# Query products of RWKV-7 moved into the state steps, the second head pair in the other half of its output, scores of two pairs in one run

## The chip, the cores and the metric

The kernel runs on one core of a Trainium2 chip. The metric is the device time of one execution in microseconds. Three executions of the kernel before took 2675.3, 2671.83 and 2676.13 us, median 2675.3 us. TensorE is called PE below, VectorE DVE, ScalarE ACT, GpSimdE POOL and SyncE SP.

## The reference, cut to what matters

One decoder layer on 2048 tokens of width 1024 in float32: an RMS norm, one input projection, two mixers side by side (HGRN2 on four heads of 128, RWKV-7 on eight heads of 64), an output projection, and a ConvFFN. The change lies in the RWKV-7 mixer. Per head it computes

```python
def step(S, inp):
    rt, wt, kt, vt, at, bt = inp
    sa = jnp.einsum('bhvk,bhk->bhv', S, at)
    S = S * wt[:, :, None, :] + sa[..., None] * bt[:, :, None, :] + vt[..., None] * kt[:, :, None, :]
    y = jnp.einsum('bhvk,bhk->bhv', S, rt)
    return S, y
...
mu = jnp.mean(y, axis=-1, keepdims=True)
var = jnp.mean(jnp.square(y - mu), axis=-1, keepdims=True)
y = ((y - mu) * lax.rsqrt(var + RW_GN_EPS)).reshape(B, T, RW_WIDTH)
y = y * ln_w.astype(f32) + ln_b.astype(f32)
bonus = jnp.sum(heads(r * k * r_k.astype(f32)), axis=-1, keepdims=True) * heads(v)
y = y + bonus.reshape(B, T, RW_WIDTH)
return (y * g).astype(out_dtype)
```

`S` is a head's 64 by 64 state, `rt` the query, `ln_w` and `ln_b` the weight and bias of the group norm over a head's 64 channels.

## The kernel before

**Blocks and streams.** The tokens are cut into four blocks of 512. Phase 1 (projections and mixers, up to about 1345 us of the trace) is made of three Python generators: `dense` (the input and output projections, f32r products of 128 by 128 by 512 in triples at lines 263 to 265, named `pj`), `rw_super` (RWKV-7; eight calls, one for each block and each half of the heads) and `hg_unit` (HGRN2). One tick of the loop advances `rw_super` and `hg_unit` to their next `yield` and then lets `dense` issue about 2000 ns of work. So a `yield` in `rw_super` is a place where some nine dense matmuls go in. The framework then reorders the instructions of each engine a little by its own estimates, and each engine works through its queue in that order. Phase 2 (the last block's output projection, ConvFFN, final norm) has nothing of this.

**One call of `rw_super`** handles four heads, as two pairs `u` = 0, 1 of 128 channels each; a head `h` of a pair lies in partitions 64h to 64h+63. The 512 tokens are eight chunks of 64. The stages with the lines that the prediction names:

- L723, the scores: for each pair 16 small products (64 rows, 128 columns out, 128 tokens) in two groups `j`, each followed by a mask product on DVE (L726) into `M` and by a `yield` for each pair.
- L737 and L740 send pieces of `M` through DRAM into the layout `E`; L792 and L794 are 31 steps of a triangular inverse on DVE, L798 and L804 its transposes (`TZ`, `TTs`); L811, L824 and L837 bring the inverse together on PE.
- L857 starts the state sums `xp` in PSUM. L871 makes the chunk transition `G` and changes the queries `RT`. L871 walks over all four 64 by 64 quarters of the array: its `tile_position` is (64 or 0, 0 or 64).
- L884 starts the output sums `yp` in PSUM with the products inside a chunk.
- L894, the state steps: for each of eight chunks four products of `G` with the state `XH`, then DVE multiplies the result by the decay (L896) into the next `XH`, then a `yield`. The steps are a chain through DVE.
- L904, the query products: after the last step, 32 products of the states with `RT` are added into `yp`. Head `h` uses the quarter (64h, 64h).
- The group norm: square on ACT, two sums by the matrix `group` (L1060, L1061), Ln and Exp on ACT, one product on DVE (L916), then one ACT operation per pair with `ln_w` and `ln_b` (L918), the bonus `BV` (L926), the gate (L925 and L927) and the store to `oT` (L928).

A run below is a stretch of small matmuls on PE between two dense ones. An f32 matmul leaves two records in the trace, so a run of eight matmuls is shown as x16. The profile names PSUM tiles by their pools: `rw` for those of `rw_super` (`xp` and `yp` among them), `hg` for HGRN2 (L1032 is its state product).

**The start.** Before phase 1 all small parameter vectors are loaded as rows and transposed into `vt` (L153), and the first block's rows are normed: for each of four row tiles `nsq` and two `nst` operations on ACT (L118), then a product on DVE (L150), transposes on PE (L257), and `hh` and `hl` from them. Casts of the first weights (`wh`, L247) stand in the same ACT queue.

Of the kernel before, what the change touches and what calls it, by code (L numbers as in the profile page):

```python
# [7 lines left out]
F32 = mybir.dt.float32  # L8
# [3 lines left out]
AF = mybir.ActivationFunctionType  # L12
# [6 lines left out]
P = 128  # L19
# [45 lines left out]
def tile_layer(ctx, tc, consts, x, norm1_w, w_in, hg_lb_logits, hg_norm_w, rw_shift_mu, rw_w0, rw_w2,  # L65
# [4 lines left out]
    V, S, TE = nc.vector, nc.scalar, nc.tensor  # L70
    dma, store = nc.sync.dma_start, nc.gpsimd.dma_start

    cp = ctx.enter_context(tc.tile_pool(name="cp", bufs=1, reuse_waits="tile"))
# [36 lines left out]
    def act(out_, in_, func, **kw):  # L110

        want = tables.get(func)
        if want is not None and want != tab["now"]:
            pre = S.preload_act_table_set(want)
            for u_ in tab["uses"]:
                tc.add_manual_dep(pre.ins, u_.ins.name, NOSYNC, reason="table order")
            tab.update(now=want, pre=pre, uses=[])
        i_ = S.activation(out_, in_, func, **kw)  # L118
        if want is not None:
            tc.add_manual_dep(i_.ins, tab["pre"].ins.name, NOSYNC, reason="table order")  # L120
            tab["uses"].append(i_)
        return i_
# [11 lines left out]
    vt = cp.tile([P, P], F32, name="vt")  # L134
    off = {}
# [19 lines left out]
    def vec(nm, i):  # L155
        return vt[:, off[nm] + i:off[nm] + i + 1]


    lb = cp.tile([P, 12], F32, name="lb")
    lb0 = vt[:, off["lb"]:off["lb"] + 4]  # L160
# [106 lines left out]
    def phase1(c1):  # L267
# [353 lines left out]
        def last_dma(nb):  # L621

            return nc.gpsimd.dma_start if nb == NBLK - 1 else dma
# [14 lines left out]
        U = range(2)  # L638

        def rw_super(nb, s_):  # L640
# [75 lines left out]
            for j in range(2):  # L716
                for u in U:
                    s1 = bank2()
                    for i in range(4):
                        b, e = 2 * j + i // 2, i % 2  # L720
                        for h in range(2):
                            hr = slice(h * 64, h * 64 + 64)
                            TE.matmul(s1[:, h, i * P:i * P + P], KB[hr, 4 * u + b, 2 * e:2 * e + 2, :],  # L723
                                      AR[hr, u, :, 2 * b + e, :], start=True, stop=True)
                    for h in range(2):
                        V.tensor_mul(M[:, :, u, 2 * j:2 * j + 2, h, :].rearrange("p e b t -> p b e t"),  # L726
                                     s1[:, h].rearrange("p (b e t) -> p b e t", e=2, t=P),
                                     s1m.unsqueeze(1).unsqueeze(1).broadcast_to([P, 2, 2, P]))
                    yield

            E = rp.tile([P, 32, 32], F32, tag="E", name="E")
# [76 lines left out]
            for b, h, e, u in quads():  # L808
                r0 = er0(e)
# [70 lines left out]
            for u in U:  # L880
                for ch in range(8):
                    b, e = ch // 2, ch % 2
                    for h in range(2):
                        TE.matmul(yp[h * 64:h * 64 + 64, u, ch * 64:ch * 64 + 64],  # L884
                                  UV[:, 4 * u + b, e, h * 64:h * 64 + 64], M[:, e, u, b, h, 64:128], start=ch == 0,
                                  stop=False, tile_position=(0, h * 64), skip_group_check=True)
            WC2 = WC.rearrange("p (u c) t -> p u c t", u=2)
            for ch in range(8):
                b, e = ch // 2, ch % 2
                cs_ = slice(ch * 64, ch * 64 + 64)  # L890
                for u in U:
                    for h in range(2):
                        hr = slice(h * 64, h * 64 + 64)
                        TE.matmul(xp[hr, u, cs_], M[hr, 1, u, b, e, 0:64], XH[hr, u, ch, :], start=False,  # L894
                                  stop=ch == 7, tile_position=(h * 64, h * 64), skip_group_check=True)
                V.tensor_mul(XH[:, :, ch + 1, :], xp[:, :, cs_], WC2[:, :, ch].broadcast_to([P, 2, 64]))  # L896
                yield
            V.tensor_copy(Xc[:, 2 * s_:2 * s_ + 2, :], XH[:, :, 8, :])
            for u in U:
                for ch in range(8):  # L900
                    cs_ = slice(ch * 64, ch * 64 + 64)
                    for h in range(2):
                        hr = slice(h * 64, h * 64 + 64)
                        TE.matmul(yp[hr, u, cs_], XH[hr, u, ch, :], RT[hr, u, ch, :], start=False, stop=ch == 7,  # L904
                                  tile_position=(h * 64, h * 64), skip_group_check=True)
            yo = tile_("KB", [2, 2, BLK], "yo")
            y1, y2 = yo[:, 0], yo[:, 1]
            act(y1, yp, AF.Square)
# [5 lines left out]
            act(y1, b1, AF.Ln, bias=epsgn, scale=1.0 / 64)  # L914
            act(y1, y1, AF.Exp, scale=-0.5)
            V.tensor_mul(y2, yp, y1)  # L916
            for u in U:
                act(y2[:, u], y2[:, u], AF.Identity, bias=vec("lnb", prs[u]), scale=vec("lnw", prs[u]))  # L918
            yield
            while ("gd", nb) not in stage:  # L920
                yield None
# [1 line left out]
            gm = bank2()  # L923
            for u in U:
                TE.matmul(gm[:, u, :], g2[:, pc[u]], gdt, start=True, stop=True)  # L925
            V.tensor_add(y2, y2, BV)  # L926
            V.tensor_mul(y2, gm, y2)  # L927
            last_dma(nb)(oT[nb][512 + prs[0] * P:512 + (prs[1] + 1) * P, :].rearrange("(u p) t -> p u t", p=P), y2)  # L928
            done["rw2"] += 1
            yield  # L930

# [670 lines left out]
```

## Time and profile before

| | |
|---|---|
| median of three executions | 2675.3 us |
| profiled execution, its span | 2678.7 us |
| PE busy | 2595.9 us, 97% of the span |
| DVE busy | 1964.4 us, 73% |
| ACT busy | 1368.4 us, 51% |
| L904, 512 records | 18.8 us busy |
| L894, 512 records | 30.2 us busy |
| L723, 512 records | 37.9 us busy |

The profile is that of one execution, whose span lies 3.4 us above the median. A line of the timeline gives the start, the duration from the first start to the last end, the engine, the line, the operation, `out<-in`, the tile of the array in use, the moving shape and the number of records. Matmuls are pipelined, so durations overlap, and the distance between starts tells what a matmul costs its queue. A bracket at the end of a line is idle time ahead of it and who ended it.

### The profile page before, as it was taken

What the parts mean: (1) busy time and instruction counts of PE and PEld (TensorE: products, weight loads), DVE (VectorE), ACT (ScalarE), POOL (GpSimd) and SP (SyncE); (2) the same over time, 40 slices, a digit from 0 to 9 for tenths busy, and PEclk for the clock granted to TensorE, in tenths of its full rate; (3) what the DMA queues carried; (4) which work ended last, traced back from release to release, by engine and by line L of the source; (5) the groups of instructions that cost most, each with busy time, mean ns of one, the idle gap of its engine ahead of it and who ended that gap; (6) DMA issues with size and microseconds to landing.
All of it is one profiled execution on the core that took longest, in us unless ns stands there. A gap on an engine that the chain in (4) does not pass through costs nothing. (4 is left out here: it accounts for less than half of the span.)

```text
span 2678.7 us, 47929 instructions
## 1 busy us (share of the span) xinstructions
PE 2595.9 (97%) x18059; PEld 2089.1 (78%) x18059; DVE 1964.4 (73%) x3744; ACT 1368.4 (51%) x2200; POOL 383.2 (14%) x686
## 2 busy tenths in 40 slices
PE   7999999999999999999999999999999999999998
PEld 5877777777777777778778888887888888888887
DVE  4877767676567675667678789988998888676556
ACT  4556453554545455344457655456555545545444
POOL 6433222212222123222100000000000000000000
PEclk9999999999999999999999999999999999999999
DMA  8654443355643546844584458756754463898665
GB/s 301 202 164 165 163 142 116 115 162 183 201 152 115 153 157 221 277 131 129 172 287 139 138 188 262 239 172 194 260 199 150 149 203 124 318 322 280 204 193 185
DMA packets 312702, 510.54 MB, mean 191 GB/s; under 512 B 46879, under 2 KB 143509, under 8 KB 312469
## 3 DMA queue, kind: packets, MB, share of 16 engines
q1 hardware_dynamic: 257937, 329.13, 37.3%
q0 software_dynamic: 54464, 178.32, 20.4%
q8 instruction: 142, 2.33, 0.4%
q14 instruction: 91, 0.75, 0.1%
q10 hardware_dynamic: 68, 0.02, 0.0%
HBM read 373.13 MB, written 134.22 MB: 189 GB/s over the span
## 5 line engine op out<-in xcount | busy, mean ns | idle before, releaser
L263 PE MATMUL pj<-hh,wh 128*128 128x512 f32 x960 | 394.1, 411 | 6.7 <-ACT rkv L118 1.6
L264 PE MATMUL pj<-hl,wh 128*128 128x512 f32 x960 | 377.9, 394 | 0.0
L265 PE MATMUL pj<-hh,wl 128*128 128x512 f32 x960 | 377.7, 394 | 0.0
L263 PE MATMUL ua<-Bh,uwh 128*128 128x512 f32 x704 | 276.1, 392 | 3.8 <-ACT m L118 2.6
L265 PE MATMUL ua<-Bh,uwl 128*128 128x512 f32 x704 | 274.3, 390 | 0.0
L264 PE MATMUL ua<-Bl,uwh 128*128 128x512 f32 x704 | 274.1, 389 | 0.0
L263 PEld LDWEIGHTS pj<-hh,wh 128*128 128x128 f32 x960 | 181.1, 189 | 56.6 <-issue 9.1
L265 PEld LDWEIGHTS pj<-hh,wl 128*128 128x128 f32 x960 | 181.0, 189 | 39.6 <-issue 0.2
L264 PEld LDWEIGHTS pj<-hl,wh 128*128 128x128 f32 x960 | 181.3, 189 | 34.3 <-issue 0.6
L247 ACT CAST uwh<-uraw 128x512 fp32r<-128x512 f32 x220 | 135.2, 618 | 137.7 <-PE ua L264 63.3
L248 DVE TENSOR_TENSOR dal<-draw,dah 128x512 fp32r<-128x512 f32 x138 | 95.3, 690 | 111.3 <-ACT dah L247 110.0
L248 DVE TENSOR_TENSOR uwl<-uraw,uwh 128x512 fp32r<-128x512 f32 x220 | 147.5, 687 | 35.0 <-ACT uwh L247 34.9
L247 ACT CAST dah<-draw 128x512 fp32r<-128x512 f32 x138 | 85.9, 622 | 163.7 <-PE da L264 79.1
L263 PEld LDWEIGHTS ua<-Bh,uwh 128*128 128x128 f32 x704 | 132.1, 188 | 33.2 <-ACT m L118 4.8
L265 PEld LDWEIGHTS ua<-Bh,uwl 128*128 128x128 f32 x704 | 132.2, 188 | 28.1 <-DVE uwl L248 0.4
L264 PEld LDWEIGHTS ua<-Bl,uwh 128*128 128x128 f32 x704 | 132.2, 188 | 26.8
L263 PE MATMUL ud<-Bh,uwh 128*128 128x512 f32 x352 | 138.0, 392 | 0.0
L265 PE MATMUL ud<-Bh,uwl 128*128 128x512 f32 x352 | 137.0, 389 | 0.0
L264 PE MATMUL ud<-Bl,uwh 128*128 128x512 f32 x352 | 137.0, 389 | 0.0
L1472 POOL DMA_DIRECT2D gd<-y x2 | 1.1, 542 | 945.3 <-DVE y L1470 945.3
L264 PE MATMUL da<-dbl,dah 128*128 128x512 f32 x332 | 129.4, 390 | 0.3 <-DVE dbl L248 0.2
L265 PE MATMUL da<-dbh,dal 128*128 128x512 f32 x332 | 129.2, 389 | 0.0
(580 smaller groups left out, 6268.9 us busy)
## 6 DMA issues: line engine op xcount, KB each, us to landing
uraw<-in_w_up_dram SPq DMA_DIRECT2D x176, 256.0 KB, 3.3
woraw<-in_w_out_dram POOLq DMA_DIRECT2D x96, 256.0 KB, 3.4
br<-gd SPq DMA_DIRECT2D x88, 256.0 KB, 4.0
draw<-Sg SPq DMA_DIRECT2D x88, 256.0 KB, 2.8
draw<-Tw SPq DMA_DIRECT2D x88, 256.0 KB, 3.1
gd<-y SPq DMA_DIRECT2D x86, 256.0 KB, 2.8
Sg<-br SPq DMA_DIRECT2D x72, 256.0 KB, 2.1
xt<-x1d SPq DMA_DIRECT2D x32, 512.0 KB, 6.1
```

What stands on the lines that cost most here:

```text
L247: S.copy(hi, src)
L248: V.tensor_sub(lo, src, hi.bitcast(F32))
L263: TE.matmul(acc, lh, rh, start=first, stop=False, skip_group_check=skip)
L264: TE.matmul(acc, lh, rl, start=False, stop=False, skip_group_check=skip)
L265: TE.matmul(acc, ll, rh, start=False, stop=last, skip_group_check=skip)
L1472: (dma if end is None else nc.gpsimd.dma_start)(gd_[2 * h + b][fb * P:(fb + 1) * P, :], ys[0][:, b * BLK:(b + 1) * BLK])
```

## The change

Four things:

1. The `yield` of the scores stands behind both pairs of a group `j`, twice, in place of once behind each pair. The number of ticks stays.
2. The query products of a chunk stand right behind the four state products of its step.
3. Pair 1 writes its output sums `yp` into the other half of the partitions: head `h` of pair `u` goes to half `h ^ u`. This holds for L884 and for the query products, so that the four query products of a step use the four quarters of the array.
4. The group norm's last ACT operation brings pair 1 back: two operations of half height read one half of `y2` and write the other half of `y1`. Their weights and biases, swapped likewise, are copied once at the start into a small tile `lnx` by two ACT copies.

```diff
+    lnx = cp.tile([P, 4], F32, name="lnx")
+    for r0 in (0, 64):
+        S.copy(lnx[r0:r0 + 64, :], vt[64 - r0:128 - r0, off["lnw"] + 1:off["lnw"] + 8:2])
...
                         V.tensor_mul(M[:, :, u, 2 * j:2 * j + 2, h, :].rearrange("p e b t -> p b e t"),
                                      s1[:, h].rearrange("p (b e t) -> p b e t", e=2, t=P),
                                      s1m.unsqueeze(1).unsqueeze(1).broadcast_to([P, 2, 2, P]))
+                for _ in U:
                     yield
...
-                        TE.matmul(yp[h * 64:h * 64 + 64, u, ch * 64:ch * 64 + 64],
+                        c0 = (h ^ u) * 64
+                        TE.matmul(yp[c0:c0 + 64, u, ch * 64:ch * 64 + 64],
                                   UV[:, 4 * u + b, e, h * 64:h * 64 + 64], M[:, e, u, b, h, 64:128], start=ch == 0,
-                                  stop=False, tile_position=(0, h * 64), skip_group_check=True)
+                                  stop=False, tile_position=(0, c0), skip_group_check=True)
...
+                for u in U:
+                    for h in range(2):
+                        hr, c0 = slice(h * 64, h * 64 + 64), (h ^ u) * 64
+                        TE.matmul(yp[c0:c0 + 64, u, cs_], XH[hr, u, ch, :], RT[hr, u, ch, :], start=False,
+                                  stop=ch == 7, tile_position=(h * 64, c0), skip_group_check=True)
                 V.tensor_mul(XH[:, :, ch + 1, :], xp[:, :, cs_], WC2[:, :, ch].broadcast_to([P, 2, 64]))
                 yield
             V.tensor_copy(Xc[:, 2 * s_:2 * s_ + 2, :], XH[:, :, 8, :])
-            for u in U:
-                for ch in range(8):
-                    cs_ = slice(ch * 64, ch * 64 + 64)
-                    for h in range(2):
-                        hr = slice(h * 64, h * 64 + 64)
-                        TE.matmul(yp[hr, u, cs_], XH[hr, u, ch, :], RT[hr, u, ch, :], start=False, stop=ch == 7,
-                                  tile_position=(h * 64, h * 64), skip_group_check=True)
...
-            for u in U:
-                act(y2[:, u], y2[:, u], AF.Identity, bias=vec("lnb", prs[u]), scale=vec("lnw", prs[u]))
+            act(y1[:, 0], y2[:, 0], AF.Identity, bias=vec("lnb", prs[0]), scale=vec("lnw", prs[0]))
+            for r0 in (0, 64):
+                rs_ = slice(64 - r0, 128 - r0)
+                act(y1[r0:r0 + 64, 1], y2[rs_, 1], AF.Identity, bias=lnx[rs_, 2 + s_:3 + s_], scale=lnx[rs_, s_:s_ + 1])
...
-            V.tensor_add(y2, y2, BV)
-            V.tensor_mul(y2, gm, y2)
+            V.tensor_add(y1, y1, BV)
+            V.tensor_mul(y1, gm, y1)
```

In the changed kernel the lines stand a little lower: the dense triple is at 266 to 268, the scores at 726, the state steps at 899; the query products happen to be at 904 in both.

What this does to the order is shown at three places. The first is PE's queue at the scores of the second call of `rw_super` (rows of one instruction form each, `x8` means eight in a row). Before:

```order
L723 MATMUL rw<-AR,KB 128x128 x8
L263 MATMUL pj<-hh,wh 128x512
L264 MATMUL pj<-hl,wh 128x512
L265 MATMUL pj<-hh,wl 128x512
L263 MATMUL pj<-hh,wh 128x512
L264 MATMUL pj<-hl,wh 128x512
L265 MATMUL pj<-hh,wl 128x512
L263 MATMUL pj<-hh,wh 128x512
L264 MATMUL pj<-hl,wh 128x512
L265 MATMUL pj<-hh,wl 128x512
L723 MATMUL rw<-AR,KB 128x128 x8
```

With the change, from the first of the two runs on:

```order
L726 MATMUL rw<-AR,KB 128x128 x16
L266 MATMUL pj<-hh,wh 128x512
L267 MATMUL pj<-hl,wh 128x512
L268 MATMUL pj<-hh,wl 128x512
L266 MATMUL pj<-hh,wh 128x512
L267 MATMUL pj<-hl,wh 128x512
L268 MATMUL pj<-hh,wl 128x512
```

Four runs of eight score products with nine dense matmuls between them have become two runs of sixteen with eighteen between them.

The second place is PE's queue behind the last state step of the first call, where `hk` and `KT` are tiles of HGRN2. Before, the step and, nine dense matmuls later, the run of query products:

```order
L265 MATMUL pj<-hh,wl 128x512
L894 MATMUL rw<-XH,M 64x64 x4
L1021 MATMUL hg<-ident,hk 128x128 x4
L1023 MATMUL hg<-hX 64x64 x4
L263 MATMUL pj<-hh,wh 128x512
...
L264 MATMUL pj<-hl,wh 128x512
L265 MATMUL pj<-hh,wl 128x512
L904 MATMUL rw<-AR,XH 64x64 x32
L1032 MATMUL hg<-VT,KT 128x128 x4
L263 MATMUL pj<-hh,wh 128x512
```

With the change:

```order
L268 MATMUL pj<-hh,wl 128x512
L899 MATMUL rw<-XH,M 64x64 x4
L904 MATMUL rw<-AR,XH 64x64 x4
L1026 MATMUL hg<-ident,hk 128x128 x4
L1028 MATMUL hg<-hX 64x64 x4
L266 MATMUL pj<-hh,wh 128x512
...
L268 MATMUL pj<-hh,wl 128x512
L1037 MATMUL hg<-VT,KT 128x128 x4
L266 MATMUL pj<-hh,wh 128x512
```

The run of 32 is gone, and four query products stand in the step.

The third is ACT's queue at the start (`nsq` and `nst` belong to the norm of the input rows, `hh` to the first projected operand). Before:

```order
L247 CAST wh<-wraw 128x512
L118 ACTIVATE nst<-nst,eps_71 128x1
L118 ACTIVATE nsq,nst<-xt 128x1024
L118 ACTIVATE nst<-nst 128x1
L118 ACTIVATE ltmp<-ltmp 128x8
L118 ACTIVATE nst<-nst,eps_71 128x1
L247 CAST wh<-wraw 128x512
L118 ACTIVATE nst<-nst 128x1
L247 CAST wh<-wraw 128x512
L114 ACT_TABLE_LOAD
L118 ACTIVATE hh<-hg,vt 128x512 x2
```

With the change:

```order
L118 ACTIVATE nsq,nst<-xt 128x1024
L118 ACTIVATE ltmp<-ltmp 128x8
L250 CAST wh<-wraw 128x512
L118 ACTIVATE nst<-nst,eps_71 128x1
L250 CAST wh<-wraw 128x512
L118 ACTIVATE nst<-nst 128x1
L114 ACT_TABLE_LOAD
L498 CAST group<-cst 128x128
L118 ACTIVATE ones<-cst 128x128
L118 ACTIVATE hh<-hg,vt 128x512 x2
```

The last `nst` operation now stands behind both casts in place of between them, and two casts of constants have come ahead of `hh`.

More of the change, by code (lines that the diff above doesn't have):

```diff
@@ L925, in rw_super @@
                 TE.matmul(gm[:, u, :], g2[:, pc[u]], gdt, start=True, stop=True)
-            V.tensor_add(y2, y2, BV)
-            V.tensor_mul(y2, gm, y2)
-            last_dma(nb)(oT[nb][512 + prs[0] * P:512 + (prs[1] + 1) * P, :].rearrange("(u p) t -> p u t", p=P), y2)
+            V.tensor_add(y1, y1, BV)
+            V.tensor_mul(y1, gm, y1)
+            last_dma(nb)(oT[nb][512 + prs[0] * P:512 + (prs[1] + 1) * P, :].rearrange("(u p) t -> p u t", p=P), y1)
             done["rw2"] += 1
```

## The prediction

> **What bounds the kernel now.** I read the page first, then busy time by stages, then the matmul groups by line, and last TensorE's timeline around each place that the change touches.
>
> ```profile
> span 2678.7 us, 47929 instructions
> PE 2595.9 (97%) x18059; PEld 2089.1 (78%) x18059; DVE 1964.4 (73%) x3744; ACT 1368.4 (51%) x2200; POOL 383.2 (14%) x686
> ```
>
> ```profile
> 0.00:60.00 60.00, 43.51 (x185) 34.85 (x186) 28.67 (x64) 29.53 (x55) 37.87 (x67) 1.00 0.88 300
> 60.00:1290.00 1230.00, 1186.37 (x11490) 934.17 (x11492) 841.05 (x2006) 605.19 (x962) 321.88 (x577) 0.99 0.51 165
> 1290.00:1345.00 55.00, 50.19 (x591) 37.98 (x589) 37.43 (x80) 25.76 (x45) 8.26 (x15) 1.00 0.50 160
> 1345.00:2678.70 1333.70, 1315.82 (x5805) 1082.09 (x5803) 1057.22 (x1597) 707.87 (x1139) 15.15 (x28) 1.00 0.64 211
> ```
>
> The second fence is busy time by stage: length, then PE, PEld, DVE, ACT, POOL, the granted clock, DMA share, GB/s. The change sits in the mixer, which ends near 1345 us; the feed-forward behind it is untouched. From 60 to 1290 us PE is busy for 1186.4 of 1230 us (96%), DVE for 68%, ACT for 49%. PE's queue sets the pace there, so a microsecond of PE work taken out is a microsecond of time, unless PE then waits longer for somebody.
>
> PE's prices come from its timeline. First the dense projection, between whose matmuls all the others stand:
>
> ```profile
> 213.93 0.39 PE L263 MATMUL pj<-hh,wh 128*128 128x512 f32 x1
> ...
> 217.79 0.39 PE L265 MATMUL pj<-hh,wl 128*128 128x512 f32 x1
> ```
>
> These are 18 dense matmuls, so 17 steps in 3.86 us: 0.227 us each. The price of a run of small matmuls is the distance from the last dense start before it to the third dense start behind it, less three such steps (0.68 us).
>
> **The change part by part.**
>
> *Scores of both pairs in one run (L723).* A run of 16 records (eight matmuls; an f32 matmul leaves two records) and one of 32:
>
> ```profile
> 230.18 0.39 PE L265 MATMUL pj<-hh,wl 128*128 128x512 f32 x1
> 230.50 1.16 PE L723 MATMUL rw<-AR,KB 64*128 64x128 f32 x16
> ...
> 232.16 0.40 PE L265 MATMUL pj<-hh,wl 128*128 128x512 f32 x1
> ...
> 86.26 0.39 PE L264 MATMUL pj<-hl,wh 128*128 128x512 f32 x1
> 86.58 2.06 PE L723 MATMUL rw<-AR,KB 64*128 64x128 f32 x32
> ...
> 89.13 0.40 PE L264 MATMUL pj<-hl,wh 128*128 128x512 f32 x1
> ```
>
> Price of 16: 1.98 - 0.68 = 1.30 us. Of 32: 2.87 - 0.68 = 2.19 us. Two short runs cost 0.41 us more than one long one: a fixed price for leaving the full array and coming back. Counted in the instruction order of both kernels, separate runs of scores fall from 34 to 20 (13 of the 14 next to dense work). **14 x 0.41 = -5.7 us**; at least 13 of them are sure, since the run of 32 was itself measured.
>
> *The query products leave their own run (L904).* They stand with a state product behind them (L1032), whose own price is shown last:
>
> ```profile
> 191.30 0.40 PE L265 MATMUL pj<-hh,wl 128*128 128x512 f32 x1
> 191.63 2.08 PE L904 MATMUL rw<-AR,XH 64*64 64x64 f32 x64
> 193.64 1.16 PE L1032 MATMUL hg<-VT,KT 128*128 128x128 f32 x8
> ...
> 195.10 0.39 PE L265 MATMUL pj<-hh,wl 128*128 128x512 f32 x1
> ...
> 132.12 0.39 PE L265 MATMUL pj<-hh,wl 128*128 128x512 f32 x1
> 132.35 1.05 PE L1032 MATMUL hg<-VT,KT 128*128 128x128 f32 x8
> ...
> 133.70 0.39 PE L265 MATMUL pj<-hh,wl 128*128 128x512 f32 x1
> ```
>
> Together 3.80 - 0.68 = 3.12 us, L1032 alone 1.58 - 0.68 = 0.90 us, so the 64 query records cost 2.22 us. The last of them takes 0.22 us, so 63 steps fill 2.08 - 0.22 us: 0.0295 us a record, 1.89 us in all, and 0.33 us are the fixed price. Eleven such runs vanish in the order: **11 x 0.33 = -3.6 us**. Their 512 records were 512 x 0.0295 = 15.1 us.
>
> *They come back, four matmuls (eight records) in each of 64 state steps.* Each step is already a small run, so it brings no new fixed price:
>
> ```profile
> 177.99 0.39 PE L265 MATMUL pj<-hh,wl 128*128 128x512 f32 x1
> 178.31 0.45 PE L894 MATMUL rw<-XH,M 64*64 64x64 f32 x8
> ...
> 179.25 0.40 PE L265 MATMUL pj<-hh,wl 128*128 128x512 f32 x1
> ```
>
> A step costs 1.26 - 0.68 = 0.58 us. What eight more records add depends on how many quarters of the array work at once. Before, a query product of head h used quarter (h, h) for both pairs, so two quarters alternated at 0.0295 us a record. Now pair 1 uses (h, 1-h): four different quarters. The kernel has such a run, the products into G (L871), which walk all four:
>
> ```profile
> 156.76 0.69 PE L871 MATMUL rw<-M 64*64 64x64 f32 x32
> 157.27 0.65 PE L871 MATMUL rw<-KBT,M 64*64 64x64 f32 x32
> ```
>
> ```profile
> L904 PE MATMUL rw<-AR,XH 64*64 64x64 f32 x512 | 18.8, 220 | 0.0
> L871 PE MATMUL rw<-KBT,M 64*64 64x64 f32 x512 | 10.6, 221 | 0.0
> L896 DVE TENSOR_TENSOR XH<-rw,WC 128x128 f32<-128x128 f32 x64 | 18.5, 289 | 32.4 <-PE rw L894 31.7
> ```
>
> 32 records start within 0.51 us, 0.0159 us each, and by group 10.6 us stand against 18.8 us for equally many records of equal shape. I take 0.0159, the row with the same four quarters: 512 x 0.0159 = 8.1 us, **net 8.1 - 15.1 = -7.0 us**. Upper bound: no overlap at all, twice 0.0295, 30.2 us and net +15.1. Lower bound: below nothing there is no mechanism, but wholly hidden where PE waits for the step's DVE product, net -15.1.
>
> The Trainium skill, "TensorE: Matmul & The Clock Gate" (section "Wait — 56ns, not 53.3ns?"), says that matmul starts never come closer than about 25 ns however small the matmul is. By that rule 512 records cost 12.8 us (an estimate) and the move saves 2.3 us, not 7.0. The L871 rows, 15.9 ns a record, speak against it if a record is a start, and for it if two records are one start (31.8 ns), which these rows don't tell.
>
> The chain inside the steps is not lengthened by a wait: the DVE product of a step (L896) waits for the four state products, and the query products stand behind these. They can delay only the next thing on PE, a dense matmul.
>
> *The ACT tail.* Two scalings of a 512-column row become one full and two half-height ones:
>
> ```profile
> L118 ACT ACTIVATE yo<-yo,vt 128x512 f32<-128x512 f32 x16 | 12.2, 811 | 3.5 <-DVE yo L916 3.5
> L118 ACT ACTIVATE M<-rw 64x512 f32<-64x512 f32 x16 | 9.5, 593 | 0.3
> ```
>
> 12.2/16 = 0.76 us becomes 2 x 0.59 = 1.19, so +0.43 us in eight stages, 3.4 us on an engine that is busy 49%. Behind it stand two DVE products and a store; the dense work between hides it. **0**, or +3.4 if that cover were gone.
>
> *The start.* Two tiny copies on ACT reorder its queue there: the cast that now ends at 19.10 comes ahead of the last row scale.
>
> ```profile
> 17.84 0.20 ACT L118 ACTIVATE nst<-nst 128x1 f32<-128x1 f32 x1
> 18.48 0.62 ACT L247 CAST wh<-wraw 128x512 fp32r<-128x512 f32 x1 [0.44 <-DMA wraw<-in_w_in_dram]
> 20.41 1.27 ACT L118 ACTIVATE hh<-hg,vt 128x512 fp32r<-128x512 f32 x2
> 18.07 0.75 DVE L150 TENSOR_SCALAR xt<-xt,nst 128x1024 f32<-128x1024 f32 x1 [2.21 <-ACT nst L118]
> ```
>
> The scale moves from 17.84 to about 19.1, the DVE scaling (L150) behind a weight product to about 19.8 and so 1.7 us late; of that the table load ahead of hh already covers some, while two constant casts (0.4 us) now stand ahead of hh. hh starts near 21.2 in place of 20.41: **+0.8 us**, between 0 and 1.7.
>
> *Where it could stall anew.* Both pairs' scores come up to nine dense matmuls earlier, and the order pulls the next consumers forward. The tight place is L811, which needs DVE's transpose TZ:
>
> ```profile
> 1276.22 1.05 DVE L798 STREAM_TRANSPOSE TZ<-Ti 128x512 f32<-128x512 f32 x1
> 1277.35 0.75 PE L811 MATMUL rw<-TZ,M 32*32 32x32 f32 x64
> ```
>
> TZ ends 0.08 us ahead of L811: no room. Dense matmuls between the last score and L811, by stage: 139, 147, 132, 125, 129, 129, 150, 149 before; 138, 150, 141, 129, 135, 126, 172, 137 now. The last stage loses 12 (2.7 us), the sixth 3 (0.7 us); the masks of the second pair end a bit later after the last score too, some 0.6 us. I put **+4 us**, between 0 (the chain shortens as well) and 8 (twice that).
>
> Sum: -5.7 - 3.6 - 7.0 + 0.8 + 4 = **-11.5 us**. The profiled execution (2678.7) becomes 2667; it lies 3.4 us above the median, so the median of 2675.3 becomes **2664**.
>
> **The rivals.**
>
> *The quarters don't overlap in so short a group.* Eight records behind eight of the old pattern cost 0.0295 each: the term of -7.0 is 0, the sum -4.5, 2671. For it: L871's row is a long steady run, a step's is not. Against: nothing in the four products depends on each other. With the page's 25 ns it would be 2668.5, an estimate. Chance 0.14.
>
> *PE merely arrives early.* Some waits of PE are set by chains, not by its own work:
>
> ```profile
> PE rw L857 <- ACT M L118: 10.1, 7, 2.2
> ```
>
> If every stage is paced by its chain of scores, DVE inverse and state, what PE saves turns into longer waits like these and the time stays within 0.2%: 2675. Against it: the waits named on L857 are 10.1 us in all, and dense work is what fills the rest. Chance 0.12.
>
> *Slower through L811.* The order is pulled forward in every stage but the inverse is not faster: if each of eight stages waits 2.7 us as I expect of the last, that is 21.6 us against 16.3 us saved, with the start +6: 2681. It decides from 1.9 us a stage (15.5/8) on. For it: no room at TZ. Against it: five of eight stages have more dense work in between than before. Chance 0.08.
>
> *More than summed.* No new stall, and the earlier finish of the query sums shortens waits: -17, 2658. Chance 0.10.
>
> **How the numbers follow.** The forecast has 0.56. A time can be told from no change here beyond about 0.2%, 5.4 us. Faster: 0.56 + 0.10 and about 0.11 out of the first two rivals, 0.77. Same: 0.15. Slower: 0.08. The range takes in the larger gain (2658, less 2 us for the spread of single executions) and reaches to within 3 us of no change: 2656 to 2672; the likeliest case alone spans 2659 to 2669.
>
> **What would show it.** Scores in runs of 32 records with 2.2 us around them. A step of 16 records that costs 0.70 us rather than 0.58 (the quarters work) or 0.82 (they don't). No run of L904 of 64 records. A wait of PE for TZ in the last stage near 3 us, and the first dense matmul near 22.0 rather than 21.15 us. I am wrong if PE's idle time in the mixer grows by more than 10 us, or if steps grow by more than 0.25 us each.

## The result, and the profile after

Measured together, seven executions each: the changed kernel 2666.8 us median (2659.8 to 2670.3), the kernel before 2676.1 (2671.8 to 2684.0). The ratio is **0.996, interval [0.9943, 0.9976]**. Two later measurements of the changed kernel gave 0.9956 [0.9942, 0.997] and 0.9955 [0.9941, 0.9969]: by the ratios 10 to 12 us faster. The forecast was 2664.0 us, 11.5 us less than before, with a range of 2656 to 2672; the measured 2666.8 lies inside it. Three executions of the experiments at a granted clock of 0.56 to 0.85 took 2858 to 4212 us and stand in none of the ratios.

The page of the kernel after, its span and busy times:

```profile
span 2664.2 us, 47925 instructions
PE 2583.5 (97%) x18059; PEld 2085.9 (78%) x18059; DVE 1966.5 (74%) x3744; ACT 1374.6 (52%) x2210; POOL 381.6 (14%) x686
```

Its busy time by stage, with the columns of the same table of before. The mixer now ends near 1330 us in place of 1345:

```profile
0.00:60.00 60.00, 44.46 (x191) 35.41 (x192) 29.09 (x66) 30.53 (x58) 38.63 (x68) 1.00 0.87 308
60.00:1275.00 1215.00, 1173.96 (x11532) 929.60 (x11530) 842.82 (x2004) 608.44 (x967) 319.11 (x574) 0.98 0.50 166
1275.00:1330.00 55.00, 49.64 (x534) 39.38 (x534) 37.08 (x78) 25.04 (x42) 8.06 (x15) 0.94 0.51 164
1330.00:2664.20 1334.20, 1315.42 (x5806) 1081.49 (x5804) 1057.53 (x1598) 710.58 (x1145) 15.82 (x29) 1.00 0.64 211
```

The last row is the feed-forward: 1334.2 us against 1333.7, so the difference lies in the mixer. The column behind POOL's has changed too: the granted clock is 0.98 and 0.94 in the two stages of the mixer, where before it stood at 0.99 and 1.00.

For an account of the mixer I cut its span (first dense matmul to the first projection of phase 2) into windows of 1 us and split PE's time in three: busy time multiplied by the granted clock ("work"), idle time, and the rest of busy time ("lost to the clock"). One profiled execution each, in us:

| kernel | work | idle | lost to the clock | sum |
|---|---|---|---|---|
| before | 1264.5 | 48.4 | 11.3 | 1324.2 |
| changed, first profile | 1241.8 | 46.4 | 22.2 | 1310.4 |
| changed, second | 1243.9 | 46.5 | 15.9 | 1306.3 |
| changed, third | 1242.7 | 45.6 | 14.8 | 1303.1 |

Work fell by 21 to 23 us, idle time by 2 to 3, and the clock took 4 to 11 back. The profiled execution of before was longer than most of that kernel's: the time of an execution is 1.8 us above its span, so it took some 2680.5 us, against medians of 2673.1 to 2676.1. Differences between single profiles therefore overstate the gain by some 4 to 7 us.

What the change does is there in PE's timeline, first a run of scores, then a state step with its query products:

```profile
84.83 0.39 PE L267 MATMUL pj<-hl,wh 128*128 128x512 f32 x1
85.15 2.06 PE L726 MATMUL rw<-AR,KB 64*128 64x128 f32 x32
...
87.70 0.40 PE L267 MATMUL pj<-hl,wh 128*128 128x512 f32 x1
...
172.43 0.39 PE L268 MATMUL pj<-hh,wl 128*128 128x512 f32 x1
172.75 0.39 PE L899 MATMUL rw<-XH,M 64*64 64x64 f32 x6
172.93 0.27 PE L904 MATMUL rw<-AR,XH 64*64 64x64 f32 x2
172.97 0.23 PE L899 MATMUL rw<-XH,M 64*64 64x64 f32 x2
173.03 0.28 PE L904 MATMUL rw<-AR,XH 64*64 64x64 f32 x6
...
173.81 0.40 PE L268 MATMUL pj<-hh,wl 128*128 128x512 f32 x1
```

With the three dense steps, 0.68 us together, taken off, as in the prediction, the run of 32 costs 2.19 us and the step 1.38 - 0.68 = 0.70 us. These two are typical: of the runs and steps that stand alone between dense matmuls at full clock, eleven runs have a median of 2.19 us and 30 steps one of 0.70.

Three of the waits of PE in the mixer, by line (total, times, longest, in us); the first had 10.1 us before, the third 0.5:

```profile
PE rw L861 <- ACT M L118: 8.3, 5, 4.2
PE pj L266 <- ACT hh L243: 7.2, 7, 2.0
PE rw L815 <- DVE TZ L802: 2.4, 3, 2.0
```

### The profile page after: what moved, and what is told of

Its sections match the earlier page's. It is cut to its first block, busy times and chain, and to the rows that moved or that the text cites. A ratio compares the mean times of both kernels' runs of the same rounds, so it can differ in the third digit from the quotient of the medians.

```text
span 2664.2 us, 47925 instructions
## 1 busy us (share of the span) xinstructions
PE 2583.5 (97%) x18059; PEld 2085.9 (78%) x18059; DVE 1966.5 (74%) x3744; ACT 1374.6 (52%) x2210; POOL 381.6 (14%) x686
## 4 chain that ended last, share of the span: by engine, by line
PE 50%; DMA 6%; DVE 5%; ACT 3%; issue 2%; SPq 0%; DVEq 0%; POOL 0%; ACTq 0%; POOLq 0%
PE ua L266 5%; PE ua L268 5%; PE ua L267 5%; PE da L266 3%; PE da L267 3%; PE da L268 3%; PE ud L268 2%; PE ud L267 2%; PE ud L266 2%; PE pj L266 2%; PE pj L267 2%; PE db L268 2%; PE db L266 2%; PE db L267 2%; PE pj L268 2%
```

## The experiments

**One part at a time.** Four kernels, measured side by side. The first has only the merged scores:

```diff
-                    yield          # behind each pair u
+                for _ in U:        # behind both pairs
+                    yield
```

> The kernel before with the one yield edit: scores of both pairs in one run, query products as before. Fixed-price theory (my forecast): separate runs of scores fall from 34 to 20 and each saves 0.41 us, so 5.7 us of TensorE work go; with up to 4 us of new waits at L811 the time is 2 to 6 us below the kernel before, ratio 0.998 to 0.9993, and runs of 32 records cost 2.19 us. Rival, TensorE merely arrives early: ratio 1.000, TensorE's idle time in the mixer grows by some 6 us. Rival of the slowed clock (seen in the profile after): the work falls by 5.7 us, but the granted clock decides each single execution; kernels with the same work spread over about 10 us with the clock between 0.989 and 0.995.

Measured: ratio 0.9997 [0.9985, 1.0009]. The price per run was as forecast, yet no change of the time can be told: the interval reaches from 4 us less to 2 us more. PE's idle time in the profile did not grow, as the rival would have it, but fell from 48.4 to 45.7 us.

The second has everything but the other output half (so neither `lnx` nor the third ACT operation): the query products stand in the steps, on quarter (h, h).

> The changed kernel without the swap: query products in the state steps and scores in one run, but both pairs of the output sums in the same half, so a head's two query products use the same quarter; the small weight tile and the third ACT operation go too. Quarter theory: a step costs about 0.82 us in place of the 0.70 of the changed kernel and the 0.58 of the one before, 64 x 0.12 = 7.5 us more than the changed kernel; ratio to the kernel before 0.998 to 0.9995. Rival, the quarters give nothing in so short a group: a step costs the same 0.70 us, and the time is that of the changed kernel, 0.996.

Measured: 0.9966 [0.9952, 0.9979], faster than my theory said (0.998 to 0.9995) and close to the rival's 0.996. Its steps, however, cost what the theory said:

```profile
171.20 0.39 PE L265 MATMUL pj<-hh,wl 128*128 128x512 f32 x1
171.52 0.45 PE L895 MATMUL rw<-XH,M 64*64 64x64 f32 x8
171.80 0.40 PE L900 MATMUL rw<-AR,XH 64*64 64x64 f32 x8
...
172.70 0.40 PE L265 MATMUL pj<-hh,wl 128*128 128x512 f32 x1
```

1.50 - 0.68 = 0.82 us (also the median of 28 such steps), the forecast's figure for quarters that do not work. The swapped half is worth 0.12 us a step and 64 x 0.12 = 7.7 us of PE's queue. In the time it brought 0.9966 - 0.9956 = 0.1%, some 2.7 us, with intervals that overlap: the 7.7 us are shown in PE's queue, not in the time.

The third has everything but the merged scores.

> The changed kernel with the yield edit undone: query products in the steps with four quarters, scores in separate runs as before. Forecast: 3.6 us for eleven runs and 7.0 us for the quarters stay, 5.7 us are lost, so 4 to 10 us below the kernel before, ratio 0.9965 to 0.9985. Rival, TensorE merely arrives early: 1.000 here and in the run with the scores alone. If new waits come from the scores' order (L811 pulled forward), TensorE's idle time in the mixer is smaller here than in the changed kernel.

Measured: 0.9991 [0.9979, 1.0003]: 2.4 us less, where I had expected 4 to 10, and again no change that can be told. Idle time was larger here than in the changed kernel (51.9 against 46 us), so the scores' order does not bring it new waits on the whole.

> The changed kernel once more, beside the others on the same chip. Forecast theory: 0.996 as first measured. Theory of the slowed clock: its executions spread over some 10 us and follow the granted clock, about 2658 at 0.995 and 2668 at 0.990, and those of the kernel before spread likewise; at equal clock the distance is 15 us or so.

Measured: 0.9956 [0.9942, 0.997]. So the parts alone give 0.8 us (scores) and 2.4 us (queries with the other half), and both at once 11.8 us. In work the parts do add up:

| kernel | work | idle | lost to the clock | sum |
|---|---|---|---|---|
| scores only | 1256.4 | 45.7 | 10.6 | 1312.7 |
| without the other half | 1253.7 | 45.0 | 6.2 | 1304.9 |
| scores apart | 1251.4 | 51.9 | 9.9 | 1313.2 |

Scores alone take off 8.1 us of work, the rest alone 13.1, together 21.2; the whole change took off 20.6 to 22.7. What does not add up must lie in idle time and the clock, though the differences between these rows are hardly larger than what single profiles are off by. The idle time comes next.

**A wait that grew.** In the second stage PE waits for ACT's `M` 1.67 us before and 4.20 us after. It is 3.69 us with the scores merged alone and 1.93 with them apart, so it comes with the merged scores. (Over all stages this wait did not grow: 10.1 us before, 8.3 to 9.2 in the three profiles of the changed kernel.) My first theory was that dense work is missing there, since the ticks around the scores had changed. I moved one tick from the scores to the place of the wait:

```diff
-                for _ in U:
+                for _ in range(j + 1):
                     yield
...
+            yield
             for u in U:          # L861, the state sums
```

> The changed kernel, with one of the four score yields (the one behind both pairs of j = 0) taken away and one put right ahead of the state sums (L861 of the changed kernel, which wait for ACT's M). In the order, dense matmuls between L841 and L861 go from 12, 12, 12, 9, 10, 6, 12, 12 per stage to 18, 14, 18, 6, 18, 9, 10, 18, and separate tile runs from 195 to 189. Theory: the idle time that the merged scores left at L861 (4.20 us in the second stage, 8.3 us over all stages) mostly goes, and with it the stretch of lowered granted clock behind it (300 to 310 us of the trace; such an event costs 1.7 us, the half of 3.4): work at full clock in the mixer falls by a further 2 us (6 runs fewer at 0.41), idle time there by about 5, the clock's share by 2, in all 5 to 10 us below the changed kernel run beside it. Rival: the idle time is set by a chain and only moves to the next consumer (the inverse or the first state step): within 3 us of the changed kernel.

Measured: ratio 1.0013 [1.0004, 1.0022], slower than the kernel before and 15 us behind the changed kernel beside it.

> The kernel before with the scores of both pairs in one run and, as in the run with the moved yield, one of the four score yields put ahead of the state sums; the queries stand in their own run as before. Separate tile runs 202 (before 220, scores merged alone 207). Theory: what the merged scores alone did not bring (ratio 0.9997 where 5.7 us were due) was eaten by the wait at L857 and its lowered clock, so with that wait covered the time is 5 to 9 us below the kernel before. Rival: the merged scores bring nothing at all however they are covered: within 3 us of the kernel before.

Measured: 1.0062 [1.005, 1.0074], some 17 us worse than the merged scores alone (0.9997). The theory fell in both, and so did its rival, which allowed a difference of 3 us. In the first, work stayed as in the changed kernel (1242.0 us) and idle time rose to 65.9; in the second, work stayed near that of the merged scores (1255.5) and idle time rose to 61.4. PE's waits in the first of the two:

```profile
PE rw L876 <- DVE AR L882: 10.9, 5, 3.9
PE rw L862 <- ACT M L118: 8.7, 6, 2.8
...
PE rw L726 <- DVE M L729: 4.4, 6, 1.0
```

The wait for `M` did not shrink (8.7 against 8.3 us over all stages), and two new ones appeared: the scores now wait for their mask on DVE, and the second pair's `G` waits for DVE's `AR`. The tick between the score groups had covered the one; the other is explained by the next reading.

> The changed kernel once more, to stand beside the others on the same chip: 10 to 14 us below the kernel before, with stretches of lowered clock near 220, 300, 580 or 645, 920, 1120 and 1295 us if these are tied to places in the order.

Measured: 0.9955 [0.9941, 0.9969], with lowered clock at 216, 298, 575, 643, 909 and 1288 us: most of the places came back, none near 1120.

**Who holds it up.** The timeline of all engines in the second stage, before:

```profile
295.14 0.33 SPq L1055 DMA_DIRECT2D oT<-osq  x1
297.82 2.21 PE L837 MATMUL rw<-RHS,TTs 64*64 64x128 f32 x62
300.67 0.43 DVE L936 TENSOR_SCALAR hk<-hf 128x512 f32<-128x512 f32 x1 [4.12 <-DMA oT<-osq]
301.13 0.44 ACT L118 ACTIVATE hX<-hk 128x256 f32<-128x256 f32 x1 [2.07 <-DVE hk L936]
301.58 2.41 ACT L118 ACTIVATE UV<-rw 64x512 f32<-64x512 f32 x4
304.65 2.09 PE L857 MATMUL rw<-UV,KBT 128*64 128x64 f32 x64 [1.67 <-ACT M L118]
```

And after:

```profile
292.11 2.35 PE L841 MATMUL rw<-RHS,TTs 64*64 64x128 f32 x62
292.34 0.33 SPq L1060 DMA_DIRECT2D oT<-osq  x1
297.62 0.43 DVE L941 TENSOR_SCALAR hk<-hf 128x512 f32<-128x512 f32 x1 [2.87 <-DMA oT<-osq]
298.08 0.45 ACT L118 ACTIVATE hX<-hk 128x256 f32<-128x256 f32 x1 [2.37 <-DVE hk L941]
298.55 2.40 ACT L118 ACTIVATE UV<-rw 64x512 f32<-64x512 f32 x4
300.96 1.82 ACT L118 ACTIVATE M<-rw 128x512 f32<-128x512 f32 x3
301.61 3.68 PE L861 MATMUL rw<-UV,KBT 128*64 128x64 f32 x64 [4.20 <-ACT M L118]
```

Read it from below. The state sums read `UV` and `KBT`; what they wait for is that ACT's first copy into `M` empties the PSUM bank that they write. `M` stands behind `UV` in ACT's queue, and `UV` behind `hX`, which belongs to HGRN2 and has nothing to do with RWKV. `hX` waits for DVE's `hk`, and `hk` shares its buffer with `osq`, the output of the HGRN2 unit before, whose store is still under way: 5.3 us from its issue (292.34) to `hk` (297.62). The products that `UV` reads end at 300.0 us before and at 294.5 after, 5.6 us earlier; `UV` starts only 3.0 us earlier. The missing 2.5 us are the longer wait. In the kernel with the moved tick the same store holds `hk` for 4.49 us in the seventh stage, with DVE's `AR` behind it, and PE waits 3.85 us for `AR`.

Three kernels test this by taking the store's source out of that buffer. The last product goes into the gate's own tile:

```diff
-            V.tensor_mul(sq, sq, gg)
-            last_dma(nb)(oT[nb][j * P:(j + 1) * P, :], sq)
+            V.tensor_mul(gg, sq, gg)
+            last_dma(nb)(oT[nb][j * P:(j + 1) * P, :], gg)
```

> The changed kernel, with HGRN2's gated output written into the gate's own tile and stored from there, so that the next unit's hk no longer waits for the store of osq. Theory: in the second stage PE's wait for ACT's M (4.2 us) is made in ACT's queue: UV stands behind hX, hX waits 2.4 us for DVE's hk, and hk waits 2.9 us for the store of osq, while the products that UV reads had ended 4 us before. With the store out of the way DVE's waits for it (6.0 us over four places) are gone, UV starts 3 to 4 us sooner, PE's wait there falls to 1 us or less, and the lowered clock at 300 us (1.7 to 3.4 us) goes with it: 3 to 7 us below the changed kernel. Rival: UV is held by something else in ACT's queue, or the saved wait comes back at the next consumer: within 2 us of the changed kernel.

Measured: 2654.1 us median, ratio **0.9931 [0.9917, 0.9946]**, where the changed kernel has 0.9955 to 0.996. The second stage:

```profile
292.25 2.36 PE L841 MATMUL rw<-RHS,TTs 64*64 64x128 f32 x62
292.48 0.33 SPq L1060 DMA_DIRECT2D oT<-hgg  x1
292.49 0.43 DVE L941 TENSOR_SCALAR hk<-hf 128x512 f32<-128x512 f32 x1
293.68 0.44 ACT L118 ACTIVATE hX<-hk 128x256 f32<-128x256 f32 x1
296.22 2.41 ACT L118 ACTIVATE UV<-rw 64x512 f32<-64x512 f32 x4
299.30 2.09 PE L861 MATMUL rw<-UV,KBT 128*64 128x64 f32 x64 [1.72 <-ACT M L118]
```

`hk` no longer waits, `UV` starts 2.3 us earlier, PE's wait is 1.72 in place of 4.20 us (I had expected 1 us or less), and the state sums take 2.09 us rather than 3.68. What still stood ahead of `UV` in ACT's queue is the norm of the next rows, which ended at 296.20 us. This is the fastest kernel here; it was not measured beside the changed kernel, only both against the kernel before, and the intervals still overlap by a little.

> The kernel before with the scores of both pairs in one run and nothing else of the change, and HGRN2's output stored from the gate's tile. Theory: the merged scores alone brought nothing (ratio 0.9997) because the wait behind the store ate them; with it gone they bring what their runs cost: 4 to 7 us below the kernel before with the same store. Rival: what eats them is elsewhere: the two are within 2 us.

> The kernel before with HGRN2's output stored from the gate's tile, nothing else. DVE's waits for the store (6.1 us over three places) go, PE's wait for M in the second stage (1.67 us) shrinks. Both theories: 0 to 3 us below the kernel before, since the products that UV reads end late there and the store holds them up less.

Measured: 0.9967 [0.9954, 0.998] and 0.9979 [0.9967, 0.999]. So the buffer alone is worth 5.7 us on the kernel before, twice what I expected, and 7 to 8 us with the merged scores. But the two stand only 2.7 us apart, between my theory (4 to 7) and its rival (2), with intervals that overlap: the wait behind the store is a real loss in every version, and it does not by itself explain why the merged scores alone brought nothing. The profiles show where the gain lies: without the store PE's wait for `M` over all stages falls from 10.1 to 3.8 us in the kernel before, from 8.5 to 5.1 with the merged scores and from 8.3 to 5.0 in the changed kernel.

**The clock.** The other part that did not add up. In the changed kernel the clock falls near the end of that wait and stays low behind it (same columns as the table by stage):

```profile
298.00:301.00 3.00, 0.00 (x0) 0.00 (x0) 2.92 (x9) 2.86 (x6) 0.70 (x2) 0.91 0.89 324
301.00:304.00 3.00, 2.39 (x44) 2.40 (x46) 0.42 (x1) 1.74 (x3) 0.00 (x0) 0.50 0.12 45
304.00:307.00 3.00, 3.00 (x90) 2.88 (x86) 0.00 (x0) 0.00 (x0) 0.00 (x0) 0.50 0.00 0
```

To see whether the wait causes it, I gave PE something to do there:

```diff
+            if (nb, s_) == (0, 1):
+                for _ in range(56):
+                    TE.matmul(xp[:, 0, 0:P], group, ones, start=True, stop=True, skip_group_check=True)
             for u in U:          # L861, the state sums
```

> The changed kernel, with 56 constant products of 128 x 128 (the group matrix by ones, 3 to 3.5 us of PE, into the bank of the state sums, whose first products overwrite them) right ahead of L861 in the second stage alone, where PE waits 4.20 us for ACT's M. Their results are used by nothing. Theory (the granted clock falls because PE has been idle): the wait shrinks to about 1 us, the stretch of lowered clock at 300 to 310 us reads 1.00, the other stretches stay, and the time is equal or 1.7 to 3.4 us shorter although 3 us of work were added. Rival (the lowered clock has nothing to do with idle time, it comes with the work or by chance): the stretch stays at 300 to 310 us, and the time is equal or up to 3 us longer.

Measured: 0.9985 [0.9972, 0.9999], 8 us slower than the changed kernel. It tested nothing of what it was meant for, because the added products waited themselves (the view ends at 312 us, with 54 of the 56):

```profile
300.44 11.78 PE L859 MATMUL rw<-ones,group 128*128 128x128 f32 x54 [4.42 <-ACT M L118]
```

They write the bank that ACT's `M` has to empty first. So PE was as idle as before, and 12 us of work at the lowered clock (0.22 us a product) followed. It did show that the bank alone, without the data, makes PE wait as long. The second attempt writes into a bank of HGRN2 instead:

```diff
+            if (nb, s_) == (0, 1):
+                fb = bank("hg")
+                for _ in range(56):
+                    TE.matmul(fb[:, 0:P], group, ones, start=True, stop=True, skip_group_check=True)
             xp = bank2()
```

> The changed kernel, with 56 constant products of 128 x 128 ahead of L861 in the second stage alone, this time into a bank of HGRN2 that is free there; their results are used by nothing. The order puts them in place of nine dense matmuls (2.0 us), which go behind L861. At 0.11 us each they fill 6.1 us, so PE's wait of 4.2 us falls below 0.5 us and PE is given about 2 us more to do than it has idle time there. Theory (the clock falls because PE was idle): no lowered clock at 298 to 310 us, which is worth 1.7 to 3.4 us, so the time is 1.5 us shorter to 0.5 us longer than that of the changed kernel. Rival (the lowered clock belongs to the place or comes by chance): it stays there and the time is 2 us longer.

Measured: 0.9947 [0.9931, 0.9964], 2660.5 us; the changed kernel has 0.9955 to 0.996. The added products, the state sums behind them, and the clock at the same place:

```profile
294.34 6.36 PE L859 MATMUL hg<-ones,group 128*128 128x128 f32 x56
300.83 2.09 PE L865 MATMUL rw<-UV,KBT 128*64 128x64 f32 x64
```

```profile
298.00:301.00 3.00, 2.87 (x30) 2.73 (x30) 2.59 (x8) 2.93 (x6) 0.00 (x0) 1.00 0.11 42
301.00:304.00 3.00, 3.00 (x129) 2.87 (x127) 0.00 (x0) 0.98 (x2) 0.00 (x0) 1.00 0.00 0
304.00:307.00 3.00, 3.00 (x17) 2.21 (x20) 1.29 (x2) 0.00 (x0) 0.65 (x2) 1.00 0.02 5
```

The clock is 1.00 throughout, although apart from the added products, and nine dense matmuls that now stand behind the state sums, nothing changed there: `hk` still waits 2.94 us for the store, `hX` 2.44 us for `hk`. 6.4 us of added work cost nothing that can be measured. The other profiles say the same of this place: in all six in which PE idled 3.7 to 4.4 us ahead of the state sums the clock fell at its end, in the eight others (1.9 us of idle time or less) it did not. At this place the lowered clock is caused by PE's idling.

## Why the prediction came out right, and where that was luck

*Scores in one run, -5.7.* The price was right to the hundredth (2.19 us for 32 records). Work fell by 8.1 us when this was done alone. But its time hardly fell (0.8 us), so as a term of time it is not shown for this part alone. In the second stage the gain ran into the store, as the rival "PE merely arrives early" describes it; I gave that rival to the whole kernel, and it held in one stage; why the time of the kernel with the merged scores alone did not fall stays open.

*Queries out of their own run, -3.6, and the quarters, -7.0.* The step cost 0.70 us as forecast, 0.82 without the swapped half. So the quarters do overlap in groups of eight records. The first rival, that they don't, is out, and with it the Trainium skill's rule from "TensorE: Matmul & The Clock Gate" (section "Wait — 56ns, not 53.3ns?") as I had applied it, with 25 ns for each record: eight records added 0.12 us to a step, 15 ns each. Whether two records count as one start in the Trainium skill's sense stays open; if they do, 30 ns for two records agrees with it.

*The sum of work.* -16.3 was forecast, 21 to 23 were measured. 25 separate runs vanished (220 to 195 in the traces, runs on the full array not counted), as forecast; between "without the other half" and the whole, work fell by 10 to 12 us where the steps alone explain 7.7. Three separate runs more in the order of the former (198 against 195, about 1 us) account for a part of the other 2 to 4 us, single profiles may for the rest.

*The start, +0.8.* Not seen. The first dense matmul stood at 20.3, 19.8 and 19.3 us in the three profiles of the changed kernel, at 21.15 in that of before, and at 20.0 with merged scores alone, which have no `lnx`. Over all profiles it lies at 19.2 to 20.7 us with the copies and at 19.9 to 21.5 without, so what they cost does not show against what else moves it. "Near 22.0" was wrong.

*New stalls at L811, +4, mostly in the last stage.* Wrong in place and in net size. A wait for `TZ` of 1.97 us came in the seventh stage (now L815), 1.62 us in the second profile and none over 0.3 us in the third; none near 3 us came in the last. Against it, before's wait of 3.44 us in the same stage, for HGRN2's `hk`, is gone. Idle time in the mixer fell by 2 to 3 us, where this term had put 4 on top. What I had not looked at is ACT's queue ahead of L857: the 10.1 us of waits there were quoted, but not followed back to the store.

*What was missing from the sum: the clock.* It had no term, though before's own table showed 0.99 in the mixer. Over the timed executions the granted clock has a mean of 0.9954 for the kernel before and 0.9916, 0.9933 and 0.9936 in the three measurements of the changed kernel. From execution to execution of the same kernel, 0.001 less goes with 1.8 us more (158 executions of the experiments, correlation -0.64). One more, of the kernel before, is left out of both figures: its time is an ordinary 2674.1 us at a recorded clock of 0.946, and with it the slope would be 0.2 us and the correlation -0.23. If the slope also holds from kernel to kernel, which no run tests, the lower clock cost the changed kernel about 3 to 7 us. The forecast was met because misses of opposite sign offset each other: 5 to 6 us more of work saved and no net stall where 4 us were put, against the clock. That the median came within 3 us is in part luck; these accounts do not close to better than a few microseconds, since before's profile is one long execution.

That would also fit the scores alone: their clock is 0.9932, 0.0022 below before's, which by this slope is 4 us of the 5 that are missing. This is inferred from means; which windows fell in the timed executions no trace shows, and their single profile loses no more to the clock (10.6 us) than that of before. With the store moved it is the same: the merged scores have 0.9937, the kernel before with the same store 0.9953.

*"Slower through L811"* and *"more than summed"* did not occur. The profiled execution lay 5.2 us above the median rather than 3.4, which compared a span with a time; the forecast does not hang on it, as the same 11.5 us come off either.

## What to carry to other kernels

Prices of runs read from one timeline held to the hundredth of a microsecond, but they are prices of an engine's queue. Before they are summed into time, follow each wait near the edit back through the queues of the other engines, also where it ends in work of another part of the program: here a store's buffer, two engines away, held RWKV's results back in ACT's queue, and two changed lines were worth as much as half the whole change. And where an engine's clock depends on its own idling, as at the wait in the second stage, a wait costs its length and then 1.7 us or more.

## What the runs showed of the hardware

**The clock comes in steps.** In fourteen profiles the mixer has 82 stretches of lowered clock. In each the loss is a multiple of 1.7 us, the half of 3.4 us: one such window at half rate, or several in a row. They stand mostly at the end of idle time of PE. Of 56 idle gaps of 1.9 to 2.3 us, 38 had one begin near their end (from 2 us ahead of it to 3 us behind); of 20 longer ones, 17; of 55 between 1.5 and 1.9 us, 13; of 177 between 0.7 and 1.5 us, 7. Within each profile the stretches begin a whole number of 3.413 us apart, to 2 ns, so the windows lie on a fixed grid, and PE's busy share in one window tells what the next is granted: below 45% the next was lowered in 48 of 50 cases, from 45 to 60% in 24 of 68, from 60 to 80% in 22 of 245, above that in 20 of 5007, all but one of these inside a stretch that had begun. So it matters where a gap lies on the grid. Ten of the stretches have no gap of 1 us that ends between 5 us ahead of their start and 2 us behind it. Six of these stand near 574 to 583 us, each behind a window that was 64 to 70% busy; what sets these apart from other windows as busy is open. The Trainium skill, "TensorE: Matmul & The Clock Gate" (section "What's actually happening"), describes this as a free-running window of 3413 ns with the clock at half rate after an idle one, and the size of the steps and their grid agree. The Trainium skill's advice to avoid idle gaps above some 3 us (same page, section "Why this matters for your kernels") is too mild for this kernel: gaps of 2 us were enough in two cases of three.

**The same matmuls at half rate.** The 64 records of the state sums in the second stage took 3.68 us in five of the six profiles with a long wait ahead of them (3.30 in the sixth, where one window was lowered and not two), and 2.09 us in all eight others: 1.6 us more for one run.

**A store holds its source until it is through, and that varies.** The store of `osq`, 256 KB, kept its buffer for 5.3 us from its issue in the second stage, with the DMA engines busy for 0.86 of that time. Of 56 stores of this output whose landing the traces show, the shortest took 2.3 us and the longest 5.1, the latter with the DMA engines busy for 0.42 of the time; what makes one long is open.
